# A hybrid decoder layer on one core: the order of all instructions from a fixed table in place of the kernel's own list scheduler

## The chip, the core and the metric

The kernel runs on one core of one Trainium2 chip. A core has TensorE (PE: matmuls, and PEld: the loads of their weights), VectorE (DVE), ScalarE (ACT), GpSimd (POOL) and SyncE (SP), which issues all of this kernel's loads and stores. Each has its own queue of instructions and takes them strictly in order; between queues, semaphores say when something is done. The metric is the device time of one execution in microseconds, lower is better.

## What is computed

One layer over 1024 tokens of width 1024, in float32. A single input projection feeds two groups of heads side by side:

```python
h = rms_norm(x, attn_norm_w);  proj = h @ w_in          # 13 column groups
# group A: 4 heads of gated DeltaNet, chunk by chunk
qkv = silu(causal_dwconv([a_q, a_k, a_v]))               # 4 taps
q, k = l2_norm(...);  beta = sigmoid(a_b);  g = -exp(a_log) * softplus(a_a + dt_bias)
#   per chunk: r = v - k S ; vnew = T r ; o = q S + att vnew ; S = S * gl + k^T vnew
o_a = rms_norm(o) * silu(a_z)
# group B: 8 heads of attention over the 256 best keys of each query
score = sum_h w[t,h] * relu(iq[t,h] . ik[s]);  idx = top_k(causal(score), 256)
o_b = softmax(rms_norm(b_q) . rms_norm(b_k)[idx] * scale) @ b_v[idx] * silu(b_z)
x = x + concat(o_a, o_b) @ w_out
x = x + (p @ w_ple) * sigmoid(rms_norm(x) @ w_ple_gate + b_ple_gate)
```

## The kernel before

**Stages.** All large products are made of three matmuls of rounded halves: `hi` x `hi`, `hi` x `lo`, `lo` x `hi`, where `lo` is what rounding took from `hi` (`mm3`). A weight tile is loaded as `raww`, copied to `hiw` by ScalarE, and its rest `low` is made by GpSimd. The stages overlap, but in the profile they lie about so:

- 0 to 60 us: `start`. The tokens are normed and turned (`front`, `turn`, `back`: `sq`, `rs`, `rp`, `xT`, `hThi`, `hTlo`), the per-layer embeddings `p` are multiplied by `w_ple` (`ple`, with `phi`, `plo` for `p`), and small columns are projected (`sm`, with `his`, `los` for their weights). Thirty transposes of the identity into the tile `xT` (`warm`) are the first work that is written for TensorE; nothing reads them.
- 60 to 240 us: the indexer. `Piq` is a projection of one of eight heads, `lg` its logits, `relu` and `score` their sum.
- 240 to 480 us: DeltaNet. The projections `Pak`, `Paq`, `Pav`, `Paz`, `Pbq`, `Pbz` run on TensorE, and between them the chunk work of four heads (`gdn_s1`, `gdn_s2`, `inverse`, `merge`): transposes `tk`, `tq`, `tv` of k, q and v, whose columns ScalarE squares and sums (`sqj`) or scales (`v`); products `pk` and `pq`; the chain of the state over eight chunks (`rec`: matmul, VectorE `r`, matmul, VectorE `vnew`, matmul, VectorE `S`); the outputs `po`, squared as `sqo`. Beside them VectorE and ScalarE look for the 256th best score by counting (`junk`, `junka`).
- 480 to 700 us: attention. `S` are scores, masked on VectorE into `P`; ScalarE takes the exponent; `pt` are transposes of `P`, split in `ph` and `pl`, and `pv` sums the values. The output projection (`oA` to `oD`) fills TensorE between them.
- 700 us to the end: the rest of the output projection and the gate `g`, whose result goes through VectorE, ScalarE, VectorE and VectorE (`gth`) and is stored.

**PSUM.** [...] A tile such as `tk` is four quarters of 128 columns in one bank: four transposes write them and four instructions read them one by one. Projections share three banks (`mm`), `lg` two, DeltaNet three (`s`) and one each for `rec` and `po`, attention two for `S`, two for `pt` and one for `pv`.

**The order.** The kernel doesn't issue its instructions as it is written. `Plan.add` records each as an `Op`, with edges to those that it must follow: it compares the regions (partitions and columns) that they read and write, so two instructions on different quarters of a bank have no edge. `Plan.run` gives each an estimated duration and latency (`price`), then runs a list scheduler forward and backward four times for each of three assumed extra latencies (`SLACK`), plays each order through with its model and keeps the best. `Plan.issue` emits the order found. There, each instruction goes through `keep_in_program_order`, which pins it behind the instruction traced before it on its engine. Below, the tile layer adds the real semaphore waits, and it does so for whole PSUM banks. All instructions are emitted from one line, so in the profile nearly all have the line L581, and one goes by the names of tiles.

Of the kernel before, what the change touches and what calls it, by code (L numbers as in the profile page):

```python
# [72 lines left out]


ROUNDS, HOLD = 4, 0.6
SLACK = (200, 300, 400)
JITTER, UNEVEN = (1, 2), 524288
# [148 lines left out]
class Op:  # L226
    __slots__ = ("i", "eng", "fn", "args", "kw", "pre", "post", "occ", "lat", "port", "bytes", "pool", "tile", "prio",
                 "start", "end", "n", "ready", "small", "parts")

    def __init__(self, i, eng):  # L230
        self.i, self.eng, self.pre, self.post = i, eng, {}, []
        self.occ = self.lat = self.bytes = 0
        self.small, self.parts = False, []
        self.port, self.pool, self.tile = False, None, None
# [10 lines left out]
class Plan:  # L245
# [42 lines left out]
    def add(self, eng, fn, args, kw):  # L288
# [40 lines left out]
        self.price(op, outs, ins)  # L329
# [11 lines left out]
    def price(self, op, outs, ins):  # L341
        n = max([x.free() for x in outs + ins], default=1)
        on = lambda x: x.t.pool is not None and x.t.pool.space is not None
        fn, kw = op.fn, op.kw
        acc = "accum_out" in kw
        if op.eng == "sync":
            o = next((x for x in outs + ins if not x.t.dram), None) or ins[0]
            op.occ, op.bytes = 400, int(np.prod(o.ix.shape)) * SIZE[o.dt]
            op.lat = 2000
        elif op.eng == "tensor":  # L350
            n, m, k = outs[0].free(), ins[0].free(), ins[0].ix.shape[0]
            op.lat = 165
            if fn == "transpose":
                op.occ = 109
            elif F32R in (ins[0].dt, ins[1].dt):
                op.occ = max(112, n / 2.4 + 16.5)
            else:
                op.occ = max(221, 4 * n / 2.4 + 8)
                if op.small:
                    op.occ = 310 + len(op.parts) * (115 if k > 32 else 17 if n <= 16 else 25)  # L360
        elif op.eng == "scalar":
            op.occ = 40 + .92 * n + (90 if isinstance(kw.get("scale"), View) else 0) + (140 if acc else 0)
            op.lat = 100
        elif op.eng == "vector":
            two = len([x for x in ins if x.free() > 1]) > 1
            ps = any(on(x) for x in outs + ins)
            if n <= 8:
                op.occ = 100
            elif "scan" in fn:
                op.occ = 40 + 2.3 * n  # L370
            elif fn in ("tensor_copy", "memset", "transpose") or (
                    fn == "tensor_scalar" and not ps and not acc and outs[0].dt != BF16):
                op.occ = 100 + .55 * n
            elif fn == "tensor_reduce":
                op.occ = 110 + .6 * n
            else:
                op.occ = 131 + .92 * n + (60 if acc and fn == "tensor_scalar" else 0)
            op.lat = 84
            op.port = two and not ps and n > 8
        else:  # L380
            two = fn == "tensor_tensor"
            op.occ = (150 if two or n > 8 else 200) + (2.15 if two else .95) * n
            if kw.get("op") == OP.pow:
                op.occ = 340 + 160 * n
            op.lat = 40
            op.port = two and n > 64
        if op.eng != "sync":
            op.lat += 40

    def run(self):  # L390
        ops = self.ops
        for b in ops:
            if b.tile and b.tile.before:
                for o in b.tile.before.ops:
                    self.edge(o, b, 2)
        for o in ops:
            for p in o.pre:
                p.post.append(o)
        left = {o: len(o.pre) for o in ops}
        line = [o for o in ops if not o.pre]  # L400
        for o in line:
            for q in o.post:
                left[q] -= 1
                if not left[q]:
                    line.append(q)
        assert len(line) == len(ops)
        first = {}
        for o in reversed(line):
            first[o] = o.occ + o.lat + o.bytes / 300 + max([first[q] for q in o.post], default=0)
        self.best = 1e12  # L410
        for self.slack in SLACK:
            for o in ops:
                o.prio = first[o]
            for k in range(ROUNDS):
                if k:
                    self.backward()
                self.forward()
                o = sorted(ops, key=lambda o: (o.start, o.n))
                t = self.score(o)
                if t < self.best:  # L420
                    self.best, order = t, o
        self.issue(order)

    def score(self, order):
        return self.play(order, 0) + sum(self.play(order, seed) for seed in JITTER) / len(JITTER)

    def play(self, order, seed):

        free = dict.fromkeys(self.ENG + ("mark",), 0.0)
        lock = {"vector": 0.0, "gpsimd": 0.0}  # L430
        pipe = 0.0
        begin, end = {}, {}
        for o in order:
            e = o.eng
            s = free[e]
            for p, k in o.pre.items():
                s = max(s, (begin if self.early(p, o, k) else end)[p])
            occ = o.occ
            if seed and e in ("vector", "scalar", "gpsimd"):
                occ *= 1 + (o.i * 40503 + seed * 30011) % 65536 / UNEVEN  # L440
            if e in lock:
                x = lock["gpsimd" if e == "vector" else "vector"] - s
                if x > 0:
                    if o.port:
                        s += x
                    elif e == "gpsimd":
                        occ += .7 * min(x, occ)
                if o.port:
                    lock[e] = s + occ
            begin[o] = s  # L450
            free[e] = s + occ
            if e == "sync":
                pipe = max(pipe, s + 1300) + o.bytes / 280
                end[o] = pipe + 700
            elif e == "mark":
                end[o] = max([s] + [end[p] for p, k in o.pre.items() if k == 2])
            else:
                end[o] = s + occ + o.lat
        self.played = begin
        return max(end.values())  # L460

    def gap(self, p, o, kind):

        return p.start if self.early(p, o, kind) else p.end

    def early(self, p, o, kind):
        if o.eng == "mark" or kind == 0:
            return True
        return p.eng == o.eng and p.eng != "sync" and (kind == 1 or p.eng == "tensor")

    def forward(self):
        ops = self.ops
        left = {}
        pend = {e: [] for e in self.ENG + ("mark",)}
        avail = {e: [] for e in self.ENG + ("mark",)}
        free = dict.fromkeys(pend, 0.0)
        pipe = 0.0
        port = {"vector": 0.0, "gpsimd": 0.0}
        other = {"vector": "gpsimd", "gpsimd": "vector"}
        for o in ops:  # L480
            left[o] = len(o.pre)
            o.ready = 0.0
            if not o.pre:
                heapq.heappush(pend[o.eng], (0.0, o.i, o))
        n = len(ops)
        while n:
            s, e = min((max(free[e], 0 if avail[e] else pend[e][0][0]), e) for e in pend if avail[e] or pend[e])
            while pend[e] and pend[e][0][0] <= s:
                o = heapq.heappop(pend[e])[2]
                heapq.heappush(avail[e], (-o.prio, o.i, o))  # L490
            o = heapq.heappop(avail[e])[2]
            if o.port and port[other[e]] > s:
                alt = next((x for x in sorted(avail[e])[:6] if not x[2].port), None)
                if alt:
                    heapq.heappush(avail[e], (-o.prio, o.i, o))
                    avail[e].remove(alt)
                    heapq.heapify(avail[e])
                    o = alt[2]
                else:
                    s = port[other[e]]  # L500
            if pend[e] and o.occ > 400:
                nxt = pend[e][0]
                if nxt[0] < s + HOLD * o.occ and nxt[2].prio > o.prio + 500:
                    heapq.heappush(avail[e], (-o.prio, o.i, o))
# [3 lines left out]
            if o.port:  # L508
                port[e] = s + o.occ
# [1603 lines left out]
```

## Time and profile before

| | |
|---|---|
| median of 3 runs | 853.82 us (853.78 to 856.3) |
| span of the profiled execution, from its first to its last instruction | 854.4 us |
| instructions | 15369 |
| TensorE clock, mean granted | 0.999 |
| data moved | 97.36 MB, mean 114 GB/s |

The profile is one execution with the hardware profiler on; it gives its span, 854.4 us, and no other time of its own, so that the span is what the sums are made against. Busy time of an engine is the union of its instructions. A matmul is pipelined: a row says 0.39 us for one of 512 columns, yet the next begins 0.23 us later. In a timeline a row has start, length, engine, line, operation, output<-inputs and shapes; brackets say how long the engine was idle before it, and which instruction's end released it.

### The profile page before, as it was taken

How to read it: one execution, taken by the hardware profiler on the slowest of the kernel's cores; microseconds unless marked ns; L12 is line 12 of the kernel's file. 1: busy time of each engine (PE TensorE's matmuls, PEld its weight loads, DVE VectorE, ACT ScalarE, POOL GpSimd, SP SyncE). 2: the span in 40 equal slices, each digit the busy share in tenths (PEclk: the TensorE clock that was granted, in tenths of full speed). 3: DMA queues.
4: the chain of work that ended last, by engine and by line, in shares of the span. 5: the costliest groups of instructions: out<-in, count | busy, mean ns of one | idle time of the engine just before them, and what ended most of it. 6: DMA issues, size and time to landing. Idle time of an engine off the chain costs nothing.

```text
span 854.4 us, 15369 instructions
## 1 busy us (share of the span) xinstructions
PE 829.4 (97%) x5163; PEld 690.4 (81%) x5163; DVE 611.3 (72%) x1427; ACT 578.5 (68%) x1284; POOL 484.5 (57%) x651
## 2 busy tenths in 40 slices
PE   7999999999999999999999999999999999999997
PEld 6887888888877778887887888867788888888785
DVE  5544636458677888899899977798977788647334
ACT  6654555545577889977898984599766677645432
POOL 3445312242366666847675685449856487568942
PEclk9999999999999999999999999999999999999999
DMA  9872211122312311331212223657434312246453
GB/s 345 274 232 94 86 38 50 50 79 77 84 39 57 102 55 53 84 102 45 97 34 76 95 87 122 215 160 252 121 104 151 101 61 76 85 127 219 148 173 110
DMA packets 79887, 97.36 MB, mean 114 GB/s; under 512 B 24225, under 2 KB 40641, under 8 KB 79681
## 3 DMA queue, kind: packets, MB, share of 16 engines
q1 hardware_dynamic: 79808, 96.40, 35.5%
q8 instruction: 40, 0.66, 0.3%
q14 instruction: 39, 0.31, 0.1%
HBM read 70.92 MB, written 25.45 MB: 113 GB/s over the span
## 4 chain that ended last, share of the span: by engine, by line
PE 72%; DVE 9%; ACT 6%; DMA 5%; POOL 4%; issue 3%; SPq 1%; ACTq 0%; DVEq 0%; POOLq 0%
PE g L581 7%; PE Piq L581 7%; PE lg L581 5%; PE Pbz L581 4%; PE Pak L581 4%; PE Pbq L581 4%; PE Paq L581 4%; PE S L581 3%; PE pt L581 3%; PE Pav L581 3%; PE pv L581 3%; PE Paz L581 3%; PE sm L581 3%; PE ple L581 2%; POOL low L581 2%
## 5 line engine op out<-in xcount | busy, mean ns | idle before, releaser
L581 POOL TENSOR_TENSOR low<-raww,hiw 128x512 fp32r<-128x512 f32 x133 | 180.0, 1358 | 164.7 <-ACT hiw L581 124.8
L581 ACT ACTIVATE hiw<-raww 128x512 fp32r<-128x512 f32 x134 | 84.0, 630 | 69.7 <-PE g L581 21.9
L581 ACT ACTIVATE junka<-score,nt 128x1024 bf16<-128x1024 int16 (+1 forms) x96 | 110.3, 1149 | 2.4 <-DVE score L581 0.4
L581 DVE TENSOR_SCALAR_CACHE_REDUCE junk<-score,cand 128x384 bf16<-128x384 f32 (+2 forms) x96 | 71.0, 740 | 1.3
L581 POOL TENSOR_SCALAR P<-P,rsum 128x128 f32<-128x128 f32 (+7 forms) x64 | 50.7, 797 | 29.9 <-DVE rsum L581 22.2
L581 ACT ACTIVATE relu<-lg 128x384 f32<-128x384 f32 (+3 forms) x80 | 38.8, 522 | 40.7 <-PE lg L581 38.0
L581 POOL TENSOR_SCALAR nt<-acca,upa 128x1 f32<-128x1 f32 x96 | 39.5, 412 | 43.9 <-ACT junka L581 42.1
L581 ACT ACTIVATE P<-P,nm,rq 128x128 f32<-128x128 f32 (+7 forms) x64 | 55.2, 863 | 11.7 <-DVE nm L581 8.9
L581 ACT ACTIVATE ph<-pt 128x512 fp32r<-128x512 f32 x72 | 41.2, 594 | 28.2 <-PE pt L581 26.4
L581 PE MATMUL S<-kst,qT 128*128 128x384 f32 (+4 forms) x192 | 59.0, 361 | 0.7 <-DVE qT L581 0.4
L581 DVE TENSOR_TENSOR pl<-pt,ph 128x512 fp32r<-128x512 f32 x72 | 47.9, 685 | 16.0 <-ACT ph L581 15.2
L581 DVE SCALAR_TENSOR_TENSOR score<-relu,sm,score 128x384 f32<-128x384 f32 (+5 forms) x42 | 42.3, 1020 | 23.2 <-ACT relu L581 23.0
L581 PE MATMUL pt<-ident,P 128*128 128x128 f32 x288 | 52.4, 273 | 1.7 <-DVE pl L581 1.7
L581 PEld LDWEIGHTS pt<-ident,P 128*128 128x128 f32 x288 | 37.3, 140 | 12.9 <-DVE pl L581 2.3
L581 PEld LDWEIGHTS S<-kst,qT 128*128 128x128 f32 x192 | 34.6, 188 | 9.1 <-DVE mx L581 2.0
L581 PE MATMUL Piq<-hThi,hiw 128*128 128x256 f32 (+1 forms) x128 | 41.6, 343 | 0.1
L581 PE MATMUL Piq<-hThi,low 128*128 128x256 f32 (+1 forms) x128 | 41.0, 343 | 0.0
L581 PE MATMUL Piq<-hTlo,hiw 128*128 128x256 f32 (+1 forms) x128 | 39.8, 342 | 0.0
L581 DVE CUSTOM_DVE_ANT_0 P<-S,score 128x384 f32<-128x384 f32 (+3 forms) x48 | 28.3, 597 | 7.0 <-PE S L581 3.6
L581 PE MATMUL pv<-ph,vst 128*128 128x512 f32 x72 | 30.3, 420 | 0.6 <-DVE ot L581 0.6
L581 DVE TENSOR_TENSOR gth<-g,rb 128x512 f32<-128x512 f32 x16 | 11.1, 691 | 27.6 <-PE g L581 23.2
L581 PE MATMUL pv<-pl,vst 128*128 128x512 f32 x72 | 29.3, 407 | 0.0
(624 smaller groups left out, 2818.4 us busy)
## 6 DMA issues: line engine op xcount, KB each, us to landing
raww<-in_w_ct_dram SPq DMA_DIRECT2D x66, 256.0 KB
raww<-in_w_out_dram SPq DMA_DIRECT2D x32, 256.0 KB
raww<-in_w_gate_dram SPq DMA_DIRECT2D x32, 256.0 KB
xt<-in_x_dram SPq DMA_DIRECT2D x8, 512.0 KB
xc<-in_xc_dram SPq DMA_DIRECT2D x8, 512.0 KB
pled<-plt SPq DMA_DIRECT2D x16, 256.0 KB
pld<-pled SPq DMA_DIRECT2D x16, 256.0 KB
out_dram<-gth SPq DMA_DIRECT2D x16, 256.0 KB
```

Source lines behind the costliest of these rows:

```text
L581: r = getattr(getattr(self.nc, o.eng), fn)(*[real(x) for x in args], **{k: real(v) for k, v in kw.items()})
```

## The change

The scheduler with its prices, its model and its constants is gone. In its place stands `TURNS`, a packed text of one number for each of the 9328 recorded operations: it says which of those not yet issued comes next. `run` unpacks it, asserts that each operation's predecessors have been issued, and hands the order to `issue`, which adds an edge from each instruction to the one before it on its engine (of the kind that fixes order and makes no wait). The recorded operations, their edges, shapes, pools and buffers are the same in both kernels.

```diff
-import heapq
+import base64
+import zlib
...
-ROUNDS, HOLD = 4, 0.6
-SLACK = (200, 300, 400)
-JITTER, UNEVEN = (1, 2), 524288
+TURNS = r"""
+c-rlH2Y6If-uF4Tm$`Fi?)2U=B~vm<CcXDgdO{#Ql+Xg9BT^I;q$UIcgwR0{6vVZQQWRYT1r=RfyDpYRbQM&VrG0~)B8#lPukZKl@7~<!&gtjh|0frK9}p
...
+"""
...
     def run(self):
         ops = self.ops
         for b in ops:
             if b.tile and b.tile.before:
                 for o in b.tile.before.ops:
                     self.edge(o, b, 2)
...
-        for self.slack in SLACK:
-            for o in ops:
-                o.prio = first[o]
-            for k in range(ROUNDS):
-                if k:
-                    self.backward()
-                self.forward()
-                o = sorted(ops, key=lambda o: (o.start, o.n))
-                t = self.score(o)
-                if t < self.best:
-                    self.best, order = t, o
+        raw = np.frombuffer(zlib.decompress(base64.b85decode("".join(TURNS.split()))), np.uint8)
+        left, order, seen = list(range(len(ops))), [], set()
+        for k in raw[:len(ops)] + 256 * raw[len(ops):].astype(int):
+            o = ops[left.pop(k)]
+            assert all(p in seen for p in o.pre)
+            seen.add(o)
+            order.append(o)
+        assert not left
         self.issue(order)
...
                 self.tc.keep_in_program_order(r)
+                if o.eng in behind:
+                    self.tc.add_manual_dep(r.ins, behind[o.eng], mybir.DependencyInfo(
+                        mybir.DependencyClass.NoSync, mybir.DependencyReason.DATA), reason="turn")
+                behind[o.eng] = r.ins.name
```

Three places show what the table moves. First TensorE's first rows, before:

```order
L581 MATMUL xT<-ident 128x128 x30
L581 MATMUL ple_0_126<-phi,hiw 128x512
L581 MATMUL ple_0_126<-plo,hiw 128x512
L581 MATMUL ple_0_135<-phi,hiw 128x512
L581 MATMUL ple_0_135<-plo,hiw 128x512
```

And now (both `ple` tiles are products of `p`, and `xT<-ident` is the identity's transpose):

```order
L497 MATMUL ple_0_119<-phi,hiw 128x512
L497 MATMUL ple_0_119<-plo,hiw 128x512
L497 MATMUL ple_0_119<-phi,low 128x512
L497 MATMUL ple_0_119<-phi,hiw 128x512
L497 MATMUL ple_0_119<-plo,hiw 128x512
L497 MATMUL ple_0_119<-phi,low 128x512
L497 MATMUL xT<-ident 128x128 x2
L497 MATMUL ple_0_131<-phi,hiw 128x512
L497 MATMUL xT<-ident 128x128 x4
```

The thirty transposes no longer stand first; they are spread among the `ple` matmuls. In the same stretch ScalarE had this order before:

```order
L581 ACTIVATE hiw<-raww 128x512
L581 ACTIVATE his<-raws 128x1088
L581 ACTIVATE hThi<-xT 128x4x128 x2
L581 ACTIVATE his<-raws 128x1088
L581 ACTIVATE plt<-ple_0_142 128x512
```

And has this one now:

```order
L497 ACTIVATE plt<-ple_0_131 128x512
L497 ACTIVATE hiw<-raww 128x512
L497 ACTIVATE hThi<-xT 128x4x128
L497 ACTIVATE his<-raws 128x1088 x2
L497 ACTIVATE plt<-ple_0_142 128x512
```

The first `hThi` has moved ahead of both halves of `his`.

Second, TensorE in the DeltaNet stage, the transposes of k of the last head (`acc_902` is k; brackets name the engine's semaphore that a row waits for), before:

```order
L581 MATMUL tk<-ident,acc_902 128x128 [waits DVE_49,PE_49,Activation_49]
L581 MATMUL Pbq_0_4382<-hTlo,hiw 128x512
L581 MATMUL Pbq_0_4382<-hThi,low 128x512
L581 MATMUL tk<-ident,acc_902 128x128
L581 MATMUL Pbq_1_4673<-hThi,low 128x512
L581 MATMUL Pbq_1_4673<-hThi,hiw 128x512
L581 MATMUL Pbq_1_4673<-hTlo,hiw 128x512
L581 MATMUL tk<-ident,acc_902 128x128 [waits Activation_49]
L581 MATMUL Pbq_1_4673<-hThi,low 128x512
```

And now (`acc_848` is the same k, `to` are transposes of an output and `wd` small products of `merge`):

```order
L497 MATMUL tk<-ident,acc_848 128x128 [waits Activation_49]
L497 MATMUL tk<-ident,acc_848 128x128
L497 MATMUL Paq_0_4861<-hThi,low 128x512
L497 MATMUL Paq_0_4861<-hThi,hiw 128x512
L497 MATMUL Paq_0_4861<-hTlo,hiw 128x512
L497 MATMUL to<-ident,o 128x128 [waits Pool_49]
L497 MATMUL Paq_0_4861<-hThi,low 128x512
L497 MATMUL to<-ident,o 128x128 x2
L497 MATMUL Paq_0_4861<-hThi,hiw 128x512
L497 MATMUL to<-ident,o 128x128
```

Two transposes stand together, and the third comes ten rows further down, behind `wd`, without a wait for ScalarE of its own.

Third, TensorE at the last step of the state chain of the first head (`rec`, from the seventh chunk to the eighth), before:

```order
L581 MATMUL rec0c_3757<-vnew,kh 128x128 [waits DVE_49]
L581 MATMUL tk<-ident,acc_917 128x128
L581 MATMUL wd<-U,T_955 64x64 [waits PE_49,Pool_49]
L581 MATMUL wd<-U,T_955 64x64 x7
L581 MATMUL po_3594<-S,yaq_906 128x128 [waits Activation_49]
L581 MATMUL po_3594<-vnew,att 128x128
L581 MATMUL rec0c_3849<-S,acc_902 128x128 [waits DVE_49]
```

And now:

```order
L497 MATMUL rec0c_3756<-vnew,kh 128x128 [waits DVE_49]
L497 MATMUL wc<-T_847,NB 64x64 [waits DVE_49,PE_49,Pool_49]
L497 MATMUL wc<-T_847,NB 64x64 x7
L497 MATMUL rec0c_3812<-S,acc_848 128x128 [waits DVE_49]
```

Between the matmul that makes the new state and the one that reads it stand eight small ones, where eight of them, a transpose and two products stood.

More of the change, by code (lines that the diff above doesn't have):

```diff
@@ new lines @@
+pPMaft_Z9sUhk#;Uhr9L8nT`OEyV|tcu*o^VlABq#Y8CJ)E8l4UVj55?Z%sCpxh8_rwvLYXJ315>ipM+(<ZTzab?T9FFaik1aT=)>w9nG%3TNtcGly&2R<
+!lB0sbAe+Frrm5<A##A3q+nj0FK8tCLxZ+iOSlg4~)#Mz0_jgs7$mAI!<q>6+*3bRcPROG`^@YpYf}X`J@M3H||Q&los*EHsXSBb{}1lVSMaZT&~WeuHl9
+H^G0ueMq=N6k9PWOgo|(Ru6{ifmJEq=JK`%Phq&Hzd!FhH2Zwbt}%C2VE$Po?VY(0E|}YY_*}>|*}A*ebvwhCI=Vl~$bH?>?^wS_YZ@CHyTY2u_{Q3XJC7
+g@0~%Up!8;r7z&j0aq4;SyXx_r53u{1sIPbBSyLR43g@$aQw%g{5k&@32LfG&4>?e0qcT=oq{TnkMDcoG~CM+L%8?$cOYloOMIGijw+yh_i-
+}37EBS)049W~zbnsG_*Dz2C6{kXTc_XSiGw`%o2FN(f+2fWnVacG5Ebh7!tu4VXgV}|j?x6c~yev_5F`?h_;gf}}nR(CJ$x>xdoYY}*fEbFk|FD4gk1NVv
@@ L80, in bcast_rows @@
+E$jfAPN^eEk>y#UBa(56ESe^8
+"""
 def bcast_rows(ap, n, parts=128):
@@ L226 @@
 class Op:
-    __slots__ = ("i", "eng", "fn", "args", "kw", "pre", "post", "occ", "lat", "port", "bytes", "pool", "tile", "prio",
-                 "start", "end", "n", "ready", "small", "parts")
+    __slots__ = ("i", "eng", "fn", "args", "kw", "pre", "pool", "tile", "small", "parts")
     def __init__(self, i, eng):
-        self.i, self.eng, self.pre, self.post = i, eng, {}, []
-        self.occ = self.lat = self.bytes = 0
+        self.i, self.eng, self.pre = i, eng, {}
         self.small, self.parts = False, []
-        self.port, self.pool, self.tile = False, None, None
+        self.pool, self.tile = None, None
 class Queue:
@@ L339, in birth @@
         return b
[L341 to L388, printed above, removed]
     def run(self):
@@ L395, in run @@
                     self.edge(o, b, 2)
-        for o in ops:
[L397 to L409, printed above, removed]
@@ L427, in play @@
[L427 to L460, printed above, removed]
@@ L462, in gap @@
[L462 to L504, printed above, removed]
-                    s, o = nxt[0], heapq.heappop(pend[e])[2]
-            o.start, o.n = s, len(ops) - n
-            free[e] = s + o.occ
-            if o.port:
-                port[e] = s + o.occ
-            if e == "sync":
-                pipe = max(pipe, s + 1300) + o.bytes / 280
-                o.end = pipe + 700
-                free[e] = max(free[e], pipe - 1500)
-            elif e == "mark":
-                o.end = max([s] + [p.end for p, k in o.pre.items() if k == 2])
-            else:
-                o.end = s + o.occ + o.lat + self.slack
-            n -= 1
-            for q in o.post:
-                q.ready = max(q.ready, self.gap(o, q, q.pre[o]))
-                left[q] -= 1
-                if not left[q]:
-                    heapq.heappush(pend[q.eng], (q.ready, q.i, q))
-        return max(o.end for o in ops)
@@ L561, in issue @@
     def issue(self, order):
-        first = {}
+        first, behind = {}, {}
         for o in order:
```

149 lines of the change are left out of this document (115 added, 34 removed).

## The prediction

> **What bounds the kernel now.** I read the page's busy table first, then TensorE's busy time stage by stage, then its waits, then the timeline at three places.
>
> The page says that TensorE is the bound and that little of it is idle:
>
> ```profile
> span 854.4 us, 15369 instructions
> PE 829.4 (97%) x5163; PEld 690.4 (81%) x5163; DVE 611.3 (72%) x1427; ACT 578.5 (68%) x1284; POOL 484.5 (57%) x651
> ```
>
> The change adds and removes no instruction, so 829.4 us stays, and what an order can win is in 854.4 - 829.4 = 25.0 us of idle time (and a little in the ends of matmuls before a wait, which count as busy). The table of stages says where it lies; each row is a stretch, with TensorE's busy time first:
>
> ```profile
> 0.00:40.00 40.00, 34.97 (x197) 30.31 (x198) 21.75 (x47) 25.55 (x50) 15.41 (x29) 1.00 0.86 312
> 80.00:240.00 160.00, 159.62 (x915) 137.32 (x914) 94.84 (x152) 85.87 (x206) 48.20 (x45) 1.00 0.22 65
> 240.00:480.00 240.00, 231.96 (x2003) 190.69 (x2001) 210.89 (x566) 206.74 (x505) 160.40 (x317) 1.00 0.24 69
> 545.00:620.00 75.00, 71.68 (x375) 56.49 (x374) 67.61 (x229) 65.72 (x151) 54.23 (x62) 1.00 0.59 185
> 620.00:700.00 80.00, 80.00 (x410) 66.97 (x409) 61.42 (x160) 54.99 (x102) 49.48 (x44) 1.00 0.33 106
> 700.00:848.00 148.00, 146.55 (x694) 119.25 (x692) 84.82 (x140) 74.15 (x127) 96.97 (x72) 1.00 0.41 134
> 848.00:855.00 7.00, 0.17 (x1) 0.00 (x0) 3.27 (x5) 1.00 (x2) 0.00 (x0) 0.84 0.20 75
> ```
>
> Idle: 5.0 us in the first 40, 8.0 in the DeltaNet stage (240 to 480), 3.3 where attention begins (545 to 620), 1.5 near the end, and about 6 us behind the last matmul. Between 80 and 240 and between 620 and 700 it is 0.4 and 0.0: there an order can win nothing and can only lose. VectorE (210.9 of 240) and ScalarE (206.7 of 240) are nearly full in the DeltaNet stage, so a hand-over to them is easily late.
>
> The waits of TensorE, first of its matmuls and then of its weight loads (us in total, times, longest), name the largest cause:
>
> ```profile
> PE tk L581 <- ACT sqj L581: 2.5, 4, 1.4
> PE po L581 <- ACT sqo L581: 0.9, 2, 0.5
> PE pk L581 <- DVE NB L581: 0.7, 2, 0.4
> PE tv L581 <- ACT v L581: 0.6, 3, 0.2
> PE rec0c L581 <- DVE S L581: 0.7, 1, 0.7
> PEld tk L581 <- ACT sqj L581: 5.7, 10, 1.8
> PEld tv L581 <- ACT v L581: 1.8, 4, 0.6
> PEld po L581 <- ACT sqo L581: 1.6, 3, 0.7
> PEld tq L581 <- ACT sqj L581: 1.3, 5, 0.4
> PEld pk L581 <- DVE NB L581: 1.2, 2, 0.6
> ```
>
> All but the `rec0c` row, which the rivals use, are writes into one quarter of a PSUM tile that wait for a read of another quarter. The plan of before has no edge for that, since it compares columns, so it puts matmuls where these waits catch them. The worst one, TensorE and then ScalarE:
>
> ```profile
> 404.99 0.39 PE L581 MATMUL Pbq<-hTlo,hiw 128*128 128x512 f32 x1
> 406.80 0.33 PE L581 MATMUL tk<-ident,acc 128*128 128x128 f32 x1 [1.42 <-ACT sqj L581]
> 405.74 0.61 ACT L581 ACTIVATE hiw<-raww 128x512 fp32r<-128x512 f32 x1
> 406.37 0.28 ACT L581 ACTIVATE sqj<-tk 128x128 bf16<-128x128 f32 x1
> ```
>
> The third transpose of `tk` stood still for 1.42 us, and all matmuls behind it, because the squares of the first two were queued on ScalarE behind other work.
>
> **The change part by part.** *The added chain of edges.* Each instruction already passes through `keep_in_program_order`, which pins it behind the one traced before it on its engine. The new edge names the same instruction and is of a kind that makes no wait, so I cost it at nothing from both sides; the table alone acts.
>
> *Waits for shared banks.* The weight loads' rows sum to 11.6 us over 24 waits, the matmuls' to 4.7. The worst wait shows what a matmul really loses: it started 406.80 - 404.99 = 1.81 us behind the one before, which is 0.23 at pace, so 1.58 was lost, against 1.8 idle on the weight load. At 0.22 less for each of 24, 11.6 comes to 6.3 us. In the two orders, rows of `tk` and `tq` that wait for ScalarE fall from 35 to 9; those of `tv` and `po` hardly fall (18 to 16), and `pk` rows with any wait rise (8 to 11). So of 5.7 + 1.3 - 15 x 0.22 = 3.7 us I expect 74% gone, 2.7; the ends are 0 (the squares come late for another reader) and 6.3 (all gone). I take 3.5, nearer the count, with something for the matmuls queued behind.
>
> *The start.* Before, thirty transposes of the identity ran while the first loads landed; now they are spread among the first `ple` matmuls, which stand first. Rows of the start (the two short windows have TensorE's time and count first):
>
> ```profile
> 1.77 5.66 PE L581 MATMUL xT<-ident 128*128 128x128 f32 x30 [1.77 <-DVE ident L581]
> 2.00:6.00 4.00, 4.00 (x20) 4.00 (x20) 1.74 (x3) 1.96 (x4) 0.00 (x0) 1.00 0.90 293
> 6.30:7.10 0.80, 0.80 (x9) 0.80 (x9) 0.04 (x1) 0.00 (x0) 0.00 (x0) 1.00 0.99 323
> 4.21 0.63 ACT L581 ACTIVATE hiw<-raww 128x512 fp32r<-128x512 f32 x1
> 7.19 0.47 PE L581 MATMUL ple<-phi,hiw 128*128 128x512 f32 x1
> 11.29 1.11 ACT L581 ACTIVATE his<-raws 128x1088 fp32r<-128x1088 f32 x1
> 12.43 1.48 DVE L581 TENSOR_TENSOR los<-raws,his 128x1088 fp32r<-128x1088 f32 x1
> 14.56 0.29 PE L581 MATMUL sm<-his,hThi 128*128 128x272 f32 x1
> 809.34 38.85 PE g L581 x166
> ```
>
> The weights were ready at 4.84, the first `ple` matmul began at 7.19: up to 2.3 us can be won. Against it: 20 transposes took 4.0 us, 9 then 0.8, so TensorE ran at about half pace for its first 4.3 us of work (the granted clock stands at 1.00 in both rows and doesn't show it); the last ten of the thirty took 1.1 us, 0.11 each. Before, this lay under the loads; now it falls on needed matmuls, a loss of 2.2. [...]
>
> Up to the first `sm` matmul the new order holds 22 `ple` matmuls (0.234 each, from 38.85 / 166), 21 of the transposes and one `rp` (0.11 each): 7.5 us, so TensorE gets there at 4.9 + 7.5 + 2.2 = 14.6. But ScalarE now has the first `hThi` ahead of `his`. `hThi` needs `rp`, which TensorE reaches at 4.9 + 12 x 0.234 + 15 x 0.11 + 2.2 = 11.5, then four products on VectorE:
>
> ```profile
> 10.38 1.53 DVE L581 SCALAR_TENSOR_TENSOR xT<-xc,gcol,rp 128x128 f32<-128x128 f32 x4 [4.04 <-PE rp L581]
> 19.58 0.50 PE L581 MATMUL ple<-phi,hiw 128*128 128x512 f32 x1 [1.49 <-ACT phi L581]
> ```
>
> 11.5 + 0.3 + 1.53 + 0.6 (`hThi`) + 1.1 (`his`) + 1.4 (`los`) = 16.4, with hops 16.6. At the second `sm` matmul TensorE is 16.6 - 7.6 = 9.0 us behind its own work. Before, at 14.56, it had done 23 x 0.234 + 31 x 0.11 = 8.8, so 5.8 behind. That is +3.2; against it before lost 1.5 later, waiting for `phi`, and about 0.5 more in small waits, which the later TensorE may not meet. I take +1.2, ends -2.3 and +3.2.
>
> *All other hand-overs.* Idle time in the three stages with any is 8.0 + 3.3 + 1.5 = 12.8, less 4.7 for banks: 8.1 us in dozens of waits under 1 us (weights, `pt`, `rec`, `S`). A plan whose times are not upset by bank waits can place these better; 80 to 240 and 620 to 700 show that idle near 0 can be reached. Rows of `rec`, `S` and `pt` that wait for VectorE fall from 228 to 204 only. Ends 0 and 8.1; I take half, 4.1.
>
> *The end.* The last two gate tiles met on VectorE:
>
> ```profile
> 848.93 0.72 ACT L581 ACTIVATE gth<-gth,bg 128x512 f32<-128x512 f32 x1 [0.66 <-DVE gth L581]
> 849.53 0.69 DVE L581 TENSOR_TENSOR gth<-gth,x 128x512 f32<-128x512 f32 x1
> 850.14 0.68 DVE L581 SCALAR_TENSOR_TENSOR gth<-gth,pld 128x512 f32<-128x512 f32 x1
> ```
>
> The last product could start at 849.65 and started at 850.14, behind the other tile's sum. In the new order seventeen matmuls (4.0 us) follow the last one of the tile before, and its 2.8 us of chain are over by then: -0.5.
>
> *Queues passed.* SyncE's loads stand in another order too, but the distance from a weight buffer's release to its next use stays above 2 us on TensorE's work, so I cost that at nothing; if a load lost its cover, a `hiw` on ScalarE (0.6) and a `low` on GpSimd (1.3) would follow it on the path.
>
> Sum: 854.4 - 3.5 + 1.2 - 4.1 - 0.5 = 847.5. The profiled execution lies 0.6 above the median of 853.8, so 846.9 us.
>
> **The rivals.** *Slower: the state chain of DeltaNet gets too tight.* In the new order the matmul that reads the new state stands nearer to the one that makes it. Rows of before give the price:
>
> ```profile
> 315.73 0.49 PE L581 MATMUL rec0c<-r,U 128*128 128x128 f32 x2
> 316.25 0.35 DVE L581 TENSOR_SCALAR vnew<-rec0c,br 128x128 f32<-128x128 f32 x1 [0.22 <-PE rec0c L581]
> 319.48 0.88 DVE L581 TENSOR_SCALAR_CACHE_REDUCE junk<-score,cand 128x640 bf16<-128x640 f32 x1
> ```
>
> From matmul to usable result it takes 0.49 + 0.03 + 0.35 = 0.9 us when VectorE is free, and up to 0.88 more when a count (`junk`) is ahead in its queue. By their own work, 9 of the 31 steps have under 1.0 us there in the new order and none before. With half a count, 0.45, lost in each of 31 x 3 hand-overs it is at most 42 us; it decides from (3.5 + 4.1 + 0.5 - 1.2) / 0.45 = 15 late ones. With 30 late: 846.9 + 13.5 = 860.4. For it speaks VectorE at 88% in that stage; against it that the longest wait of a `rec` matmul is 0.7 now (the `rec0c` row above).
>
> *No change: the gain is given back.* The bank waits go (-3.5), the start costs its full 3.2 and the other hand-overs stay as they are: 854.4 - 3.5 + 3.2 - 0.5 - 0.6 = 853.0. For it speaks that each engine does the same work; against it that idle time of 8.0 us lies in one stage.
>
> *More than forecast:* every idle microsecond of the three stages goes and the start wins: 854.4 - 6.3 - 8.1 - 2.3 - 0.5 - 0.6 = 836.6.
>
> That the change does nothing is excluded: the orders differ on every engine.
>
> **How the numbers follow.** About 0.3% (2.6 us) can be told from no change here. Forecast, 840 to 851: 0.52; more than that: 0.10; given back, within 0.3% of 853.8: 0.18; slower: 0.20. Faster is 0.52 + 0.10 = 0.62. The range runs from the best sum, 837, to 857, which is nothing won and the start at its worst (854.4 + 3.2 - 0.6); it leaves out the far end of the slower case and little else.
>
> **What would show it.** Right: no wait of `tk` for `sqj` above 0.5 us; under 5 us idle from 240 to 480; one gate tile alone at the end. The start is right if the first `ple` matmul comes near 4.9 us and the second `sm` matmul near 16.6. Wrong: idle time in 80 to 240 or 620 to 700, or `rec` rows at the head of TensorE's waits.

## The result, and the profile after

The changed kernel takes 848.88 us (median of 20 runs, 846.04 to 855.07), the kernel before 855.25 us on the same chip (20 runs, 852.95 to 858.12). The ratio is 0.9927, with a 95% interval of 0.9910 to 0.9943: faster by 6.2 us, 4.9 to 7.7. The forecast was 846.9 us, a gain of 6.9 in a range of 837 to 857. Two executions among the experiments, one of the kernel before at 2099 us and one of `new_middle2` at 1649 us, are slow runs and are left out everywhere.

The page of one execution of the changed kernel, its span and TensorE's row:

```profile
span 844.4 us, 15315 instructions
...
PE 826.2 (98%) x5163; PEld 687.6 (81%) x5163; DVE 598.6 (71%) x1427; ACT 580.0 (69%) x1284; POOL 470.1 (56%) x651
```

This execution took 846.11 us, 1.7 more than its span, and only one of the 20 was shorter. The two spans differ by 10.0 us, the two medians by 6.4: the profile shows a good run. What the runs tell of these differences stands with the experiments and behind them. The stages of that execution, with the columns of the table of stages shown before (length, TensorE busy, its weight loads, VectorE, ScalarE, GpSimd, clock, DMA):

```profile
0.00:40.00 40.00, 32.31 (x181) 26.87 (x182) 18.04 (x36) 24.41 (x45) 14.14 (x25) 1.00 0.83 301
80.00:240.00 160.00, 160.00 (x983) 138.53 (x982) 93.17 (x159) 87.37 (x213) 48.25 (x52) 1.00 0.23 72
240.00:480.00 240.00, 238.31 (x1996) 197.61 (x1995) 212.17 (x576) 214.00 (x518) 155.84 (x321) 1.00 0.25 72
480.00:545.00 65.00, 63.27 (x345) 53.57 (x344) 50.31 (x110) 42.64 (x101) 38.15 (x63) 1.00 0.40 125
545.00:620.00 75.00, 73.68 (x380) 58.60 (x378) 64.00 (x214) 64.05 (x143) 55.55 (x63) 1.00 0.54 172
620.00:700.00 80.00, 80.00 (x410) 65.52 (x410) 62.90 (x159) 55.44 (x102) 51.73 (x44) 1.00 0.35 116
700.00:838.00 138.00, 138.00 (x652) 111.59 (x651) 77.72 (x134) 70.86 (x120) 89.35 (x69) 1.00 0.43 140
```

TensorE is idle for 1.7 us in the DeltaNet stage (8.0 before), 1.3 where attention begins (3.3), 0.0 from 80 to 240 and from 620 to 838. Two stretches got worse: the first 40 us, with 7.7 in place of 5.0, and 480 to 545 us, with 1.7 in place of 0.1. The latter's row before was:

```profile
480.00:545.00 65.00, 64.86 (x362) 55.30 (x361) 48.35 (x92) 42.81 (x99) 39.88 (x62) 1.00 0.37 123
```

TensorE's waits in the changed kernel, matmuls and then the weight loads of `tk` (us in total, times, longest):

```profile
PE ple L497 <- ACT hiw L497: 4.9, 1, 4.9
PE rec3c L497 <- DVE vnew L497: 1.7, 1, 1.7
PE sm L497 <- ACT hThi L497: 1.7, 2, 1.0
PE sm L497 <- DVE los L497: 0.9, 1, 0.9
...
PE rec2c L497 <- DVE r L497: 0.3, 1, 0.3
...
PE tk L497 <- ACT sqj L497: 0.2, 1, 0.2
PE rec2c L497 <- DVE S L497: 0.2, 1, 0.2
```

```profile
PEld tk L497 <- ACT sqj L497: 0.8, 2, 0.6
```

`tk` waiting for `sqj` has gone from 2.5 to 0.2 on the matmuls and from 5.7 to 0.8 on the weight loads. The head of the list is now the first load (`hiw`), one step of the state (`rec3c`) and the start (`sm`).

To compare orders beyond idle time I use a lag. At time t it is t less the work that TensorE has begun by then, each matmul counted at the spacing that the trace shows at full pace (0.231 us for 512 columns, 0.126 for 272, 0.111 for a float32 transpose), and the thirty transposes of the identity counted as nothing. What grows is lost. It needs no equal stages, and it sees half pace and late starts, which busy time doesn't. From the traces, in us (rounded, so that a difference read from the table can be 0.1 off the one in the text):

| t | before | after | no_chain | banks_only | new_tail | no_warm | best2 |
|---|---|---|---|---|---|---|---|
| 40 | 12.4 | 14.6 | 17.6 | 12.5 | 13.1 | 14.5 | 13.2 |
| 80 | 13.2 | 14.5 | 17.4 | 13.3 | 13.6 | 14.3 | 13.0 |
| 240 | 15.4 | 15.5 | 18.4 | 14.7 | 15.8 | 15.2 | 14.3 |
| 480 | 34.5 | 26.5 | 29.4 | 29.9 | 33.1 | 26.1 | 25.0 |
| 520 | 35.6 | 28.7 | 33.6 | 30.9 | 34.2 | 30.0 | 26.9 |
| 838 | 44.6 | 35.0 | 39.8 | 39.9 | 40.9 | 36.4 | 34.6 |

Before against after: the start is 2.3 worse at 40 us and 0.1 at 240, since from 40 to 240 the old order lost 3.1 and the new one 0.9. The DeltaNet stage to 520 us is better by 6.9 (20.1 lost against 13.2), attention and gate by 2.6 (9.0 against 6.4), and the end by 0.5.

### The profile page after: what moved, and what is told of

Same layout as the page of the kernel before. It is cut to its first block, busy times and chain, and to the rows that moved or that the text cites. A ratio compares the mean times of both kernels' runs of the same rounds, so it can differ in the third digit from the quotient of the medians.

```text
span 844.4 us, 15315 instructions
## 1 busy us (share of the span) xinstructions
PE 826.2 (98%) x5163; PEld 687.6 (81%) x5163; DVE 598.6 (71%) x1427; ACT 580.0 (69%) x1284; POOL 470.1 (56%) x651
## 4 chain that ended last, share of the span: by engine, by line
PE 87%; DVE 5%; ACT 4%; DMA 2%; issue 1%; POOL 1%; SPq 0%; ACTq 0%; DVEq 0%; POOLq 0%
PE g L497 11%; PE Piq L497 8%; PE lg L497 6%; PE Pbz L497 5%; PE Paz L497 5%; PE Paq L497 5%; PE Pav L497 4%; PE S L497 4%; PE Pak L497 4%; PE pv L497 4%; PE pt L497 4%; PE Pbq L497 3%; PE sm L497 3%; PE ple L497 3%; PE Pik L497 1%; PE po L497 1%
## 5 line engine op out<-in xcount | busy, mean ns | idle before, releaser
L497 ACT ACTIVATE hiw<-raww 128x512 fp32r<-128x512 f32 x134 | 83.6, 628 | 44.4 <-DMA raww<-in_w_gate_dram 15.5
L497 POOL TENSOR_SCALAR P<-P,rsum 128x128 f32<-128x128 f32 (+7 forms) x64 | 48.5, 763 | 42.0 <-DVE rsum L497 27.7
L497 ACT ACTIVATE relu<-lg 128x384 f32<-128x384 f32 (+3 forms) x80 | 41.2, 522 | 41.7 <-PE lg L497 35.6
L497 ACT ACTIVATE P<-P,nm,rq 128x128 f32<-128x128 f32 (+7 forms) x64 | 55.2, 864 | 13.3 <-DVE nm L497 8.8
L497 PE MATMUL S<-kst,qT 128*128 128x384 f32 (+4 forms) x192 | 61.0, 367 | 0.4 <-DVE qT L497 0.3
L497 PE MATMUL pt<-ident,P 128*128 128x128 f32 x288 | 59.6, 274 | 0.9 <-DVE pl L497 0.6
L497 DVE SCALAR_TENSOR_TENSOR score<-relu,sm,score 128x384 f32<-128x384 f32 (+5 forms) x42 | 42.5, 1025 | 16.2 <-ACT relu L497 16.0
L497 PE MATMUL Piq<-hThi,low 128*128 128x512 f32 (+1 forms) x128 | 43.3, 344 | 0.0
L497 PE MATMUL Piq<-hTlo,hiw 128*128 128x512 f32 (+1 forms) x128 | 41.7, 343 | 0.0
L497 PE MATMUL Piq<-hThi,hiw 128*128 128x512 f32 (+1 forms) x128 | 41.5, 343 | 0.0
L497 PEld LDWEIGHTS S<-kst,qT 128*128 128x128 f32 x192 | 34.6, 190 | 7.4 <-DVE mx L497 1.1
L497 PE MATMUL lg<-khi,qlo 128*128 128x384 f32 (+3 forms) x80 | 28.9, 362 | 0.0
```

What stands on the lines that cost most here:

```text
L497: r = getattr(getattr(self.nc, o.eng), fn)(*[real(x) for x in args], **{k: real(v) for k, v in kw.items()})
```

## The experiments

All times stand against the kernel before, run on the same chip in the same session (its medians there: 856.1 for the first four kernels, 856.4 for the next four, 856.3 for the last four).

| | median us (runs) | ratio to before, 95% interval |
|---|---|---|
| changed kernel | 848.88 (20) | 0.9927 (0.9910 to 0.9943) |
| no_chain | 851.13 (6) | 0.9929 (0.9906 to 0.9952) |
| banks_only | 851.73 (9) | 0.9957 (0.9940 to 0.9973) |
| old_middle | 856.56 (12) | 1.0001 (0.9985 to 1.0017) |
| warm_first | 849.50 (6) | 0.9913 (0.9891 to 0.9934) |
| old_start | 848.57 (6) | 0.9916 (0.9893 to 0.9939) |
| new_middle | 858.86 (12) | 1.0031 (1.0015 to 1.0048) |
| no_warm | 846.67 (6) | 0.9896 (0.9876 to 0.9916) |
| best | 847.94 (6) | 0.9911 (0.9892 to 0.9931) |
| new_tail | 853.46 (8) | 0.9968 (0.9954 to 0.9983) |
| new_middle2 | 857.22 (11) | 1.0015 (0.9999 to 1.0031) |
| wait_fix | 849.46 (6) | 0.9916 (0.9899 to 0.9934) |
| best2 | 844.69 (4) | 0.9868 (0.9850 to 0.9886) |

**no_chain: the table without the chain.**

```diff
-                if o.eng in behind:
-                    self.tc.add_manual_dep(r.ins, behind[o.eng], ... reason="turn")
-                behind[o.eng] = r.ins.name
```

> The changed kernel without the added edges from each instruction to the one before it on its engine; the table stays. Theory (the table alone acts): as the changed kernel, 6.4 us below the kernel before (848.9), within 0.3%. Rival (the chain holds an order that would otherwise move): off by more than 2.6 us in either direction. As the order is the same, its trace is also a second look at the changed kernel.

Measured: 0.9929, the changed kernel's 0.9927; within 2 us the chain does nothing to the time, and TensorE's 5163 rows stand in the same order in both traces. Its trace is a second one of the same order, and its span is 849.2, not 844.4. The lag shows where the 4.8 us went: 2.9 by 40 us, and 2.1 more between 480 and 520. First the start. In the changed kernel's trace and then in this one, the second `phi` on ScalarE, and matmuls on TensorE:

```profile
5.14 0.63 ACT L497 ACTIVATE phi<-praw 128x512 fp32r<-128x512 f32 x1 [0.29 <-DMA praw<-in_pT_dram]
...
8.98 0.48 PE L497 MATMUL ple<-plo,hiw 128*128 128x512 f32 x1
9.29 0.39 PE L497 MATMUL ple<-phi,low 128*128 128x512 f32 x1
9.53 0.39 PE L497 MATMUL ple<-phi,hiw 128*128 128x512 f32 x1
...
14.73 0.39 PE L497 MATMUL sm<-his,hThi 128*128 128x272 f32 x1
16.05 0.39 PE L497 MATMUL sm<-los,hThi 128*128 128x272 f32 x1 [0.93 <-DVE los L497]
```

```profile
6.51 0.63 ACT L497 ACTIVATE phi<-praw 128x512 fp32r<-128x512 f32 x1 [1.43 <-DMA praw<-in_pT_dram]
...
7.19 0.80 PE L497 MATMUL ple<-phi,hiw 128*128 128x512 f32 x1 [0.41 <-ACT phi L497]
...
11.93 0.63 PE L497 MATMUL ple<-plo,hiw 128*128 128x512 f32 x1
12.35 0.63 PE L497 MATMUL ple<-phi,low 128*128 128x512 f32 x1
12.78 0.63 PE L497 MATMUL xT<-ident 128*128 128x128 f32 x2
```

In the first, matmuls are 0.24 apart from 9.29 on: half pace for some 4 us. In the second a load came 1.4 us later, TensorE waited 0.41 at 7.19, and matmuls are still 0.42 apart at 12.35: nearly 8 us at half pace. In the trace of old_middle, which begins in the same order, it was 5.5 (from 4.98 to 10.53), with a wait of 0.62. In that of wait_fix, of the same order too and with no wait above 0.2 there, TensorE had begun 14 matmuls by 10 us, where the changed kernel had begun 18; so the late load alone doesn't set the length, and what does isn't shown. With the old order the half pace lies over transposes that nothing needs (before: 20 of them took 4.0 us, the next 9 0.8); they end at 7.43, so that by my estimate a load as late as no_chain's, with `phi` done at 7.14, is hidden with it.

Then the second place: the DeltaNet stage's last chunk, in the trace of no_chain (windows of 2 us; the clock is the third number from the right):

```profile
486.00:488.00 2.00, 1.13 (x7) 1.08 (x8) 1.95 (x6) 0.40 (x4) 0.00 (x0) 0.97 0.67 240
488.00:490.00 2.00, 2.00 (x9) 1.71 (x7) 0.97 (x3) 1.75 (x5) 0.40 (x2) 0.50 0.00 0
490.00:492.00 2.00, 2.00 (x9) 1.71 (x10) 1.33 (x2) 1.88 (x4) 1.92 (x4) 0.68 0.02 4
```

Behind a wait of 1.71 us for `vnew` the granted clock is 0.50 for 3.4 us, which costs 1.7 us. In the profiled run of the changed kernel the same wait, 1.73 us, ended at 483.58 and the clock stayed at 1.00.

**banks_only: the old order, with only the shared-bank waits taken out.** Where a read of a PSUM tile stood ahead of a write to the same tile within 40 turns, and the write didn't depend on it, it was put behind:

```diff
+        for b in [o for o in order if o.tile and o.tile.pool.space is not None]:
+            use = sorted((o for o in b.tile.ops if o is not b), key=at.get)
+            for r in [o for o in use if o.eng != "tensor"]:
+                for w in [o for o in use if o.eng == "tensor" and at[r] < at[o] < at[r] + 40]:
+                    if r not in w.pre and w not in r.pre and not leads(r, w):
+                        r.pre[w] = 0
...
+        order = self.settle(order, at)
```

> The order of before as a table, in which only reads of a shared PSUM bank are moved behind the transposes that follow within 40 turns; waiting rows of tk and tq fall from 35 to 7, of tv and po from 18 to 13, of pk from 8 to 5. Theory A (waits for shared banks are a cost of their own, 6.7 us of TensorE's lag in the trace of before): about 5 us below the kernel before, 850. Rival B (they cover other waits, and the gain came from many better hand-overs): at most 1.5 us below it.

Measured: 0.9957, 3.7 us below before (2.3 to 5.1). TensorE's 5163 rows stand in the same order as in the trace of before, so that only the other engines' places differ. What is left of these waits, on the weight loads:

```profile
PEld po L519 <- ACT sqo L519: 1.1, 2, 0.6
...
PEld tk L519 <- ACT sqj L519: 0.5, 1, 0.5
```

Theory A holds, with less than its 5 us; B's 1.5 us lie outside the interval. The waits are a cost of their own, and about six tenths of the lag that stood at such waits in the DeltaNet stage of before, some 6 us by a count in its trace, come back as time. The gain lies where they were: the lag from 240 to 520 grows by 16.2 in place of 20.1.

**old_middle, new_tail, new_middle and new_middle2: one stage in the other order.** The first turns of the one table are taken up to a mark, then those of the other that are still open, and so on; the marks are turns.

```diff
+        old, cut = self.unpack(OLD), (2480, 5600, 9328)
+        new, seen, part = order, set(), []
+        for k, source in zip(cut, (new, old, new)):
+            take = [o for o in source[:k] if o not in seen]
+            part += take
+            seen.update(take)
+        order = part
```

new_tail has the marks (5600, 9328) with (old, new), new_middle (2480, 5600, 9328) and new_middle2 (1700, 6080, 9328), both with (old, new, old).

> The changed kernel's order to 235 us and from 505 us on, the order of before between them (the DeltaNet stage). Theory (the gain lies in this stage: TensorE's lag there grew by 19.1 us before and 11.0 after): most of the gain is gone, 853 to 856. Rival (start, attention and gate carry half): 851 to 852.

> The order of before up to 505 us (turn 5600), the changed kernel's order from there. Theory (attention, gate and end carry a smaller part: TensorE's lag from 520 us to 838 us grew by 9.0 before and 6.4 after, and 0.5 behind the last matmul): 2 to 3.5 us below the kernel before. Rival (nothing of the gain is there, as the time of old_middle seemed to say): within 1 us of it.

> The order of before, except between 235 and 505 us, where the changed kernel's order stands. Theory (the whole net gain is in the DeltaNet stage: the lag there grows by 20.1 us before and 13.2 after): 5.5 to 8 us below the kernel before, 847 to 850. Rival (attention, gate and end carry a good part of it): 3 to 4 us below it.

> As new_middle with the joints where they break no queue: the changed kernel's order from 160 us (turn 1700) to 546 us (turn 6080), the order of before around it. Theory (the first try was spoiled by its joints, a wait of 3.6 us at 514 and two of 1.7 together at 240, not by the stage): 5.5 to 8 us below the kernel before. Rival (the stage gains only together with the new start): at most 2 us below it.

Measured: old_middle is at 1.0001, all of the gain gone, a little above what was expected: its trace is 3.8 us behind that of before at 40 us and still 2.0 at 240, which hides what the tail wins. new_tail is at 0.9968, 2.7 us below before (1.5 to 3.9), as expected: attention, gate and end carry their part. Both new_middle kernels missed: 1.0031 and 1.0015 where 5.5 to 8 us of gain stood. Their traces show losses at the joints. In new_middle and then in new_middle2, a matmul of TensorE from the one order meets a VectorE queue from the other:

```profile
514.30 0.49 PE L624 MATMUL rec3c<-r,U 128*128 128x128 f32 x2 [3.62 <-DVE r L624]
```

```profile
245.13 0.43 PE L624 MATMUL kT<-ident,k 128*128 128x128 f32 x1 [1.53 <-DVE k L624]
```

Behind both, the clock fell to 0.50, from 515.2 and from 245.2 us on. In the profiled runs a mean granted clock of 0.997 or less went with such a fall ahead of the last matmul (see the last section): all 12 runs of new_middle have one so low, and 10 of 11 of new_middle2. Inside the stage, away from the joints, the lag follows whichever order stands there: from 320 to 480 us it grows by 10.5 before, 7.3 after, 7.1 in new_middle, 7.3 in new_middle2 and 11.3 in old_middle. So the traces show a part of the stage's own. A time comes from two other kernels: old_start, below, and new_tail both have the old start and the new tail, and differ only between 80 and 505 us. They stand at 0.9916 and 0.9968, which is 4.4 us (2.1 to 6.8) for the new order there, so the stage doesn't need the new start to gain; a part of new_middle2's loss beside its joints can't be excluded.

**old_start and warm_first: the old start.** old_start has the marks (900, 9328) with (old, new). warm_first leaves the new order and takes the thirty transposes, with what they need, to its front:

```diff
+        need = [o for o in order if o.eng == "tensor" and o.fn == "transpose" and o.args[1].t is o.args[2].t]
+        for o in need:
+            need += [p for p in o.pre if p not in need]
+        order = [o for o in order if o in need] + [o for o in order if o not in need]
```

> The order of before up to about 80 us (turn 900), the changed kernel's order from there. Theory (the new start is a loss: TensorE's lag at 40 us is 12.4 and 12.5 in two traces with the old start, 14.6, 16.2 and 17.6 in three with the new one): 2 to 4 us below the changed kernel, 845 to 847, 9 to 11 below the kernel before. Rival (what the start loses is given back before 240 us, as in the first pair of traces, 15.44 against 15.49): within 1 us of the changed kernel.

> The changed kernel with the thirty transposes of the identity back at the front. Theory (the half pace of TensorE's first 4.4 us of work falls on needed matmuls): the first ple matmul begins near 7.2, the second sm matmul near 15.0 in place of 16.05, the lag at 40 us falls by 1.5 and the time by 1 to 2 us against the changed kernel (847 to 848). Rival (the start is set by the order of hThi and his on ScalarE, or the loss is given back later): within 0.5 us of the changed kernel.

Measured: 0.9916 and 0.9913 against 0.9927, a gain of about 1 us that the intervals don't separate from none. old_start fits its rival and not the 2 to 4 us of its theory; warm_first's time fits its theory, but not the steps that were to bring it, since its lag at 40 us is 15.0, no better than 14.6. The start's loss is in the traces (lag at 40 us of 14.6, 17.6, 16.2 and 15.9 in four with the new start, 12.3 to 13.1 in six with the old one, and 14.1 in that of old_start itself, where the clock fell to 0.50 from 21.9 us on, behind a wait of 1.49 us for `phi`). About 2 us of it are given back by 240 us: 2.2 of 2.3 in the changed kernel's trace, and 2.2 of 5.2 in no_chain's. In warm_first the second `sm` matmul came at 16.83, not near 15: TensorE waited 1.26 and 0.98 us for `rs` and `low`, and the clock fell there too, to 0.50 from 13.7 us on.

**no_warm: without the thirty transposes.** The result leaves nothing out that another instruction reads.

```diff
+            if o.eng == "tensor" and o.fn == "transpose" and o.args[1].t is o.args[2].t:
+                continue
```

> The changed kernel without the thirty transposes of the identity, whose result nothing reads. Theory (between needed matmuls they are pure cost, 24 of them ahead of the second sm matmul, 0.11 to 0.21 us each): the transpose rp comes near 9.5 in place of 11.2, and the kernel is 1 to 2 us below the changed one. Rival (they fill waits, and keep the clock up): no gain, or up to 2 us slower because the half pace lasts longer.

Measured: 0.9896, 2.6 us better than the changed kernel's ratio, the two intervals just overlapping. The transpose `rp` came at 11.39, not 9.5: it waited 0.67 for `rs`, so the freed time was not on that path. The direction of the theory holds, its mechanism does not; where the gain comes from is open.

**best and wait_fix: the wait for the state.** The queue of VectorE in the changed kernel, and the matmul that waits for it:

```profile
481.46 0.87 DVE L497 TENSOR_SCALAR_CACHE_REDUCE junk<-score,cand 128x640 bf16<-128x640 f32 x1
482.25 0.08 DVE L497 DVE_READ_ACCUMULATOR junk<-score,cand 128x1 f32 x1
482.25 0.95 DVE L497 TENSOR_TENSOR_SCAN cum<-eq 128x384 f32<-128x384 bf16 x1
483.12 0.14 DVE L497 TENSOR_SCALAR need<-acc 128x3 f32<-128x3 f32 x1
483.18 0.34 DVE L497 TENSOR_SCALAR vnew<-rec3c,br 128x128 f32<-128x128 f32 x1
...
483.58 0.49 PE L497 MATMUL rec3c<-vnew,kh 128*128 128x128 f32 x2 [1.73 <-DVE vnew L497]
```

This is the mechanism of the slower rival: 0.34 us of work for the state stands behind 2.0 us of count, scan and sum. best puts the three behind `vnew` (on top of old_start); wait_fix, whose edit follows, puts the count behind `vnew` and the others behind the copy `S` (on the changed kernel):

```diff
+        for a, b in ((5258, 5235), (5288, 5257), (5284, 5257)):
+            at[ops[a]] = at[ops[b]] + .1
+        order = self.settle(order, at)
```

> As old_start, and on VectorE one vnew (its matmul ends near 480.9 us in the changed kernel) is moved ahead of a count, a scan and a small sum that stood before it, which made TensorE wait 1.73 us for it. Theory (that wait is on the path): 1.5 to 1.9 us below old_start, and no rec row among TensorE's waits above 0.5 us. Rival (what follows is late anyway): within 0.5 us of old_start.

> The changed kernel; on VectorE at about 482 us one vnew goes ahead of a count, and the copy of the state S ahead of a scan and a sum, so that TensorE's one wait of 1.73 us for rec3c goes. Theory (that wait costs itself and, in the traces where the granted clock fell to 0.50 for 3.4 us behind it, 1.7 more): 1.5 to 3 us below the changed kernel, and no clock below 1.00 between 480 and 495 us. Rival (the next step of the state is late instead): within 0.7 us.

Measured: 0.9911 against old_start's 0.9916, and 0.9916 against 0.9927; neither is a gain that can be told from none. The wait moved. In best TensorE waits 1.4 us for `S`; in wait_fix, one step later, for `r`:

```profile
487.07 0.35 DVE L521 SCALAR_TENSOR_TENSOR r<-rec3c,neg_eg,v 128x128 f32<-128x128 f32 x1
...
487.47 0.49 PE L521 MATMUL rec3c<-r,U 128*128 128x128 f32 x2 [1.20 <-DVE r L521]
```

The rival holds: the next step is late instead. In wait_fix's trace VectorE has no pause from 482.9 to 487.4 us, so there was no room to move this work into. The clock stayed at 1.00 in both traces, as expected, but not in every run: the mean granted clock is 0.996 or 0.997 in 5 of 6 runs of best and 2 of 6 of wait_fix.

**best2: wait_fix, no_warm and ScalarE's start together.** The first two squares go ahead of copies that wait for TensorE, the first `his` ahead of `hThi`, its `los` ahead of `hTlo`:

```diff
+        for a, b in ((185, 143), (200, 204), (202, 206), (211, 171)):
+            at[ops[a]] = at[ops[b]] - .1
```

> wait_fix and no_warm together, and at the start the first squares (sq) ahead of a copy that waits for TensorE, the first his ahead of hThi, and its los ahead of hTlo. Theory (each of the three start waits moves): second sm matmul near 15 in place of 16.3, 1 to 3 us below no_warm, 844 to 845.5. Rival (the loads set the start): within 0.7 us of no_warm apart from the wait at 482 us.

Measured: 844.69 us, 0.9868: 11.3 us below before, and below the changed kernel with intervals apart. The page, and the second `sm` matmul:

```profile
span 842.7 us, 15256 instructions
...
PE 824.4 (98%) x5133; PEld 684.3 (81%) x5133; DVE 598.0 (71%) x1427; ACT 580.5 (69%) x1284; POOL 470.8 (56%) x651
```

```profile
15.29 0.28 PE L525 MATMUL sm<-los,hThi 128*128 128x272 f32 x1
```

It came at 15.29 in place of 16.29 in no_warm, and the lag at 40 us is 13.2 in place of 14.5. Against no_warm the intervals touch, so the time of the ScalarE moves alone isn't shown. All four runs, 844.44 to 845.76 us, have a mean granted clock of 0.998; in no_warm three of six are at 0.996 or 0.997.

## Why the prediction was right, point by point

The chain, the shared banks and the end came as forecast, the start within its range and the other hand-overs at twice the forecast. That the sum came within 0.7 us of the measured gain is in part luck: the spans differ by 10.0 where the sum took 6.9 off, since that one term was too small, and the medians keep only 6.4 of it, for which no term stood.

*The bound.* I held TensorE's 829.4 us of busy time as fixed, with only 25.0 us of idle time to win. It is 826.2 now, so 3.2 of the 10.0 us came out of what counts as busy.

*The chain: nothing.* no_chain shows none, within 2 us.

*Shared banks: -3.5.* banks_only measured -3.7 (-2.3 to -5.1). The mechanism and the size are shown, though the count was off on the way: I expected three quarters of the `tk` and `tq` waits to go and `tv` and `po` to stay, and nearly all went in the changed kernel (in banks_only `po` keeps 1.1 of 1.6). No matmul of `tk` waits more than 0.2 us for `sqj` now, though one of its weight loads waits 0.6, just over the 0.5 of the first sign; the second, under 5 us of idle time from 240 to 480, is 1.7.

*The start: +1.2, ends -2.3 and +3.2.* The steps came as worked out: first `ple` matmul at 4.91 (4.9 forecast), first `sm` at 14.73 (14.6), second at 16.05 (16.6), half pace for some 4 us (4.3). The lag at 40 us was 2.3 worse, and 3 to 5 worse in the other traces: "a loss of 2.2" from half pace took its length as fixed, and it lasted some 4, 5.5 and nearly 8 us in three traces of this start (the changed kernel, old_middle, no_chain). I also put the 1.5 that before lost later, waiting for `phi`, as won back at once, but the new order waits 1.7 for `hThi` in its place. What came back came between 40 and 240 us (2.2 in the profiled run), more than half of it beyond 80, where I had said that an order can win nothing. Busy time hid what the lag shows from 80 to 240: 2.3 us lost before and 1.0 after. In no_chain's trace 3.0 us of loss stay at 240. In time, the new start costs 0.9 us against old_start, which can't be told from nothing.

*Other hand-overs: -4.1, ends 0 and -8.1.* Mis-sized, towards the far end: this is the term that was furthest off. In the profiled pair, banks and start apart, 8.1 us went (10.0 + 2.3 - 3.7 - 0.5). Of that, 2.6 are attention and gate, where new_tail measured 2.7 with the end; about 3.0 are in DeltaNet (16.2 for banks_only, 13.2 after), and 2.2 us are what the start's loss gave back from 40 to 240 us; the rest, 0.3, is within what banks_only's time and lag differ by and rounding. Counted with the start, the 2.2 leave it at nothing and the other hand-overs at under 6, still more than 4.1. The new wait of 1.73 us for `vnew` is already taken off in these sums.

*The end: -0.5.* Right. The last gate tile is alone, and each of its four steps follows the one before:

```profile
838.63 0.69 DVE L497 TENSOR_TENSOR gth<-g,rb 128x512 f32<-128x512 f32 x1 [1.07 <-PE g L497]
839.35 0.72 ACT L497 ACTIVATE gth<-gth,bg 128x512 f32<-128x512 f32 x1 [3.24 <-DVE gth L497]
840.11 0.69 DVE L497 SCALAR_TENSOR_TENSOR gth<-gth,pld 128x512 f32<-128x512 f32 x1 [0.79 <-ACT gth L497]
840.83 0.69 DVE L497 TENSOR_TENSOR gth<-gth,x 128x512 f32<-128x512 f32 x1
```

*From profile to median.* I took off 0.6, span against median. But a run takes longer than its span (846.11 against 844.4), and before's span of 854.4 is longer than two of its three runs, so that its profiled run can only be that of 856.3, 2.5 above that median. Between the 10.0 of the spans and the 6.4 of the medians, about 1 us is that before's profiled run was a long one (856.3 against 855.25), and 2.8 that the changed kernel's was a short one (846.11 against 848.88). The clock's fall doesn't explain this by itself: both profiled runs escaped it, and the mean granted clocks of the single runs show falls in both kernels, in about 30 of 55 runs of before (median 857.0, the others at 855.3) and in 11 of the 26 runs of the new order, no_chain's included (851.7, the other 15 at 847.5). What else makes the new order's runs with a fall 4 us longer, more than the 1.7 of one fall, is open.

*The rivals.* The slower one was real in kind: one late `vnew`. It needed fifteen such hand-overs; the list of waits after shows three rows of `rec`, one wait each, 2.2 us together. Behind the first load a `rec` row is indeed at the head of that list, which I had named as a sign of being wrong: the sign was badly chosen, since one wait of 1.7 us can stand there while all others are gone. No change, given back: the banks' gain stayed, and about a third of what the two spans show isn't in the medians (6.4 of 10.0 is left). More than forecast: the profiled run of 846.11 is far from its 836.6.

What stays open is how the 6.2 us of the medians divide beyond the banks (3.7) and the tail with the end (2.7), which already add up to them. The 4.4 us from old_start and new_tail for 80 to 505 us (2.1 to 6.8) hold the banks' 3.7 and leave little for the rest of DeltaNet, and the start comes out near nothing; these intervals are too wide to say more.

## What to carry to other kernels

Tell the planner how the layer below really orders accesses: an order made for quarters of a PSUM tile, while the waits go by whole banks, cost 3.7 us here, and moving the reads behind the writes won it back with TensorE's order unchanged. Compare two orders by TensorE's lag behind its own work and not by busy time, and look at a second profile of the same kernel before explaining a difference of 1%. Work that nobody needs covered the half pace where it stood ahead of the first load (in warm_first the `ple` matmuls are 0.23 apart from 7.66 us on, in the changed kernel 0.43 up to 7.63); whether it wins time there isn't shown (warm_first 0.9913 against 0.9927), and spread among needed work it was probably better left out (no_warm 0.9896).

## What the runs showed of the hardware

The clock's fall behind a wait was not expected at this size. Seven traces have a wait of 1.7 us (1.8 in no_warm) for `vnew` between 480 and 490 us. In five of them the granted clock then falls to 0.50 for 3.4 us, which at half the clock costs 1.7 us: from 484.4 us in no_warm, 486.1 in old_start, 487.9 in no_chain, 488.2 in warm_first, 1.0 to 1.6 us behind the wait, and between 490 and 495 in new_middle2. In two (the changed kernel, new_middle) it stays at 1.00. The length of a wait alone doesn't decide: the clock fell behind 1.53 us in new_middle2 (245 us), 1.49 for `phi` in old_start (20 us), and two waits of 0.44 and 0.26 in warm_first (386 and 388 us; 0.50 from 389.2), and it stayed at 1.00 behind 1.73 in the changed kernel, 1.49 for `phi` in before, 1.42 for `tk` in before and 1.4 for `S` in best. What does decide isn't shown, and no run was made to find it. So a wait of 1.7 us cost 1.7 more in five traces and nothing more in two.

The half pace at the start, in contrast, doesn't show in the granted clock: in no_chain's trace the row reads 1.00 from 5 to 15 us, while matmuls are 0.43 us apart at 11.50 to 12.35.

A run's mean granted clock tells of falls too, without a trace. By the 3.4 us at 0.50, one fall takes 0.002 from the mean of a run of 850 us. Of the 14 profiled runs, the six with a fall ahead of the last matmul have a mean of 0.993 to 0.997 (no_chain, warm_first, old_start, new_middle, no_warm, new_middle2), the eight without one 0.998 to 1.000, with what the falls behind the last matmul take (from 841.6 us on in the changed kernel, whose mean is 0.998). I read the single runs by that: 0.997 or less as a fall before the last matmul; 0.998 or more, by the 0.002, doesn't exclude one.
